# Moving elementwise work between three engines: layer 0's mixers, the S5 state exchange and layer 1's qkv

## The chip, the cores and the metric

One core of one Trainium2 chip runs the whole program. The metric is the device time of one execution in microseconds (us). The core has a matrix engine (TensorE, PE in the profile; its weight loads are PEld), a vector engine (VectorE, DVE), an activation engine (ScalarE, ACT), a general engine (GpSimd, POOL) and a queue that issues most transfers (SyncE, SP). Each takes its own instructions in program order; they meet at semaphores.

## The reference

Two layers of a transformer-like trunk run on 1024 latent tokens and 256 context tokens of width 1024. Layer 0 has one input projection that feeds two mixers, an S5 state-space scan and a gated linear attention (GLA), both in both directions; layer 1 has grouped-query attention with rotary positions. Each layer ends in a squared-ReLU MLP of width 4096.

```python
def even_mixer(h, ...):                       # layer 0
    u, q, k, v, r, glr = split(h @ w_in)      # S5 input, GLA q/k/v/r, gate rank
    s5  = s5_bidir(u, ...)                    # hs[t] = lam_bar * hs[t-1] + b_bar @ u[t], both ways
                                              # y = Re(C @ hs) + d*u ; g = gelu(y) ; g * sigmoid(g @ w_glu + b)
    gla = gla_bidir(q, k, v, r, glr, ...)     # g = log_sigmoid(glr @ w_gate2 + b)/16, chunks of 64:
                                              # b = cumsum(g); o = (q e^b) S + tril((q e^b)(k e^-b)^T) v
                                              # S = S e^bl + (k e^(bl-b))^T v ; rms_norm(o) * silu(r)
    return concat(s5, gla) @ w_out
# layer 1: q,k,v = h @ w_qkv; rms_norm, rope on latents; softmax over latent + context keys; @ w_o
# both:    x += gate * mixer ; x += gate * (relu(h @ w1)**2 @ w2)
```

## The kernel before

**Numbers.** All matrix products are made from two-part operands: `hi`, a copy of x in a narrower format (ACT writes it), and `lo = x - hi` (an elementwise subtraction). A dense product is three passes, hi·hi, lo·hi, hi·lo (L404 to L406), so every weight and every activation needs its subtraction before PE can take it. `wload` (L226 to L238) loads a weight (SP, L235), makes hi (ACT, L236) and lo (L237); by default lo is made on POOL, and its callers in `mixer_half`, `mixer_out` and the first group of `qkv` ask for DVE. `split` (L381) alternates POOL and DVE, `affine` (L388) has POOL in three of four.

**Layer 0 up to its output projection.** The token tiles are 512 + 512 latent and 256 context tokens. Independent pieces of work are written as generators and are interleaved with the dense projections of qk, v, r and glu; a list scheduler then fixes the order of every engine's instructions before the run.

- S5: tables (`s5_tables`, L652 to L681: products on DVE L652 to L654 and on POOL L656 to L658, stored to `cld` and `kd`), input products (`s5_in`, complex products by `cmul` L415 to L422, every third on POOL; L755 to L761), then the scan. In the scan every eighth state column is chained serially (`s5_chain`, 38 steps of three small DVE instructions, L813, L817, L818), and the columns between are filled by `s5_join` (one product L790 and two additions L795 for each call of 40 columns). There are eight pairs (un, d) of joins; in the last, (3, 1), POOL does them with a temporary `tm2`, in the other seven DVE with `tmp`.
- S5 output (`s5_out`): per un, loads issued by POOL (L855 to L858), an exchange of state quarters for each d (ACT L863, DVE L864, ACT L865), products L880 and L882, gelu L884, a store to `gd`, and the glu projection.
- GLA: `gla_gates` makes for each of 4 groups and 3 token tiles the decay tiles: matrix product L1000, ACT L1002, L1004, L1005, DVE L1003, POOL L1006, a DVE scan (L1009 or L1011), ACT exponentials L1014 to L1016 and L1019, DVE L1017 and L1020, POOL L1021 and L1022, stores to `qkd` and `wkd`. `gla_first` loads `wkd` back, transposes (L1067), multiplies (L1078) and accumulates the chunk states on DVE (L1091); `gla_second` makes the outputs (L1191 to L1197, one product L1196 on POOL).

Weights of the dense projections rotate through a ring of three buffers; a weight is loaded only when the product three loads back is finished. The first weight of the output projection (`w_out_e`, tile number 274) follows the glu weights in that ring.

**Layer 1.** `qkv` loads nine weight groups and applies `rope_tile` (L1735 to L1742: shuffle, product on POOL L1740, product and sum on DVE L1741, L1742). The MLP-down weights (L1463) and the attention's splits keep their POOL instructions in both versions.

Of the kernel before, what the change touches and what calls it, by code (L numbers as in the profile page):

```python
# [222 lines left out]
    s.A.free(*s.wr)  # L223


def wload(s, src, n=1024, eng=None, own=False):  # L226

    nc = s.nc
    hi, lo = [s.A([n], F32R) for _ in range(2)] if own else (s.wr[0](), s.wr[1]())
    st = s.A.f32(lo)  # L230
    shp = list(src.shape)
    dst = st[:, :n]
    if len(shp) == 3:
        dst = dst.rearrange("p (a b) -> p a b", a=shp[1])
    nc.sync.dma_start(dst, src)  # L235
    nc.scalar.activation(hi[:, :n], st[:, :n], AF.Copy)  # L236
    (eng or nc.gpsimd).tensor_tensor(lo[:, :n], st[:, :n], hi[:, :n].bitcast(F32), OP.subtract)  # L237
    return hi, lo  # L238


# [140 lines left out]
def split(s, hi, lo, src, k=0):  # L381

    nc = s.nc
    nc.scalar.activation(hi, src, AF.Copy)
    (nc.gpsimd if k % 2 else nc.vector).tensor_tensor(lo, src, hi.bitcast(F32), OP.subtract)


def affine(s, t, a, b, hi, lo, k):  # L388

    nc = s.nc  # L390
    nc.scalar.activation(hi, t, AF.Identity, bias=b, scale=a)  # L391
    nc.vector.tensor_scalar(t, t, a, b, OP.mult, OP.add)
    (nc.vector if k % 4 == 0 else nc.gpsimd).tensor_tensor(lo, t, hi.bitcast(F32), OP.subtract)  # L393


def dense(s, w, kt, act, n, off=0, mw=128, ms=128, kind="mm"):
# [135 lines left out]
def s5_prep(s):  # L532
# [61 lines left out]
    w1, w2 = A([16, 16], top=True), A([16, 16], top=True)  # L594
    for d in range(2):
        cfb = [cf[:, i, 16 * d:16 * d + 16, None].to_broadcast([128, 16, 16]) for i in range(2)]
        cmul(nc.gpsimd, Bb[:, 0, 16 * d:16 * d + 16], Bb[:, 1, 16 * d:16 * d + 16], cfb,
             [t.B[:, 0], t.B[:, 1]], w1, w2)

    s.pin = A([2, 32, 8])  # L600
# [36 lines left out]
def s5_tables(s):  # L637
# [6 lines left out]
    for st in range(8):  # L644
        un, b = divmod(st, 2)
        CL = cl()
        for d in range(2):
            g0 = 16 * d + 2 * st
            P = [s.pout[:, j, g0:g0 + 2, :, None].to_broadcast(sh) for j in range(2)]
            C = [s.Ct[:, j, 2 * st:2 * st + 2, None, :].to_broadcast(sh) for j in range(3)]  # L650
            e = nc.vector
            e.tensor_tensor(tw[0], P[1], C[1], OP.mult)  # L652
            e.tensor_tensor(CL[:, 0, d], P[0], C[0], OP.mult)
            e.tensor_tensor(CL[:, 0, d], CL[:, 0, d], tw[0], OP.subtract)  # L654
            e = nc.gpsimd
            e.tensor_tensor(CL[:, 1, d], P[0], C[2], OP.mult)  # L656
            e.tensor_tensor(tw[1], P[1], C[0], OP.mult)
            e.tensor_tensor(CL[:, 1, d], CL[:, 1, d], tw[1], OP.subtract)  # L658
        for j in range(2):
            nc.sync.dma_start(s.cld[un][64 * j:64 * j + 64, 1152 * b:1152 * b + 1152]  # L660
                              .rearrange("p (e x) -> e p x", e=2), CL[:, j].rearrange("p d g k c -> p (d g k c)"))
        yield 1.0
        tb = tab()
        pd = []
        for d in range(2):
            p = ps(s, "sp")
            nc.vector.memset(p[:, 0:128], 0.0)
            pd.append(p)
            for q in range(4):
                e, g2 = q % 2, q // 2  # L670
                h = slice(64 * e, 64 * e + 64)
                for j in range(2):
                    nc.tensor.matmul(p[32 * q:32 * q + 16, 0:128], s.Bb[h, j, 16 * d + 2 * st + g2, :],
                                     CL[h, j, d, g2, d:d + 8].rearrange("p a b -> p (a b)"),
                                     start=(j == 0), stop=(j == 1))
        nc.scalar.activation(tb[:, 0:112], pd[1][:, 0:112], AF.Copy)
        nc.scalar.activation(tb[:, 112:240], pd[0][:, 0:128], AF.Copy)
        k0 = tb[:, 112:128]
        nc.vector.tensor_tensor(k0, pd[1][:, 112:128], k0, OP.add)
        nc.vector.scalar_tensor_tensor(k0, s.eye16, s.dsk[:, st:st + 1], k0, OP.mult, OP.add)  # L680
        nc.sync.dma_start(s.kd[un, b], tb)  # L681
        yield 1.0
# [11 lines left out]
def s5_in(s):  # L694
# [12 lines left out]
    def weights(g2):  # L707
        wt, t1, t2 = wtr(), tr[0](), tr[1]()
        a = [pin[:, j, :, g2, :, None].to_broadcast(sh) for j in range(2)]
        b = [Bb[:, j, :, g2, None, :].to_broadcast(sh) for j in range(2)]  # L710
        cmul(nc.gpsimd if g2 % 3 == 0 else nc.vector, wt[:, 0], wt[:, 1], a, b, t1, t2)
        return wt

    def transposes(g2, wt):
# [25 lines left out]
    for g2 in range(16):  # L740
# [9 lines left out]
        for d in range(2):  # L750
# [6 lines left out]
            if d == 0:  # L757
                nc.scalar.activation(H[0][:, g2, :, 1:160], pv[:, :, 0:159], AF.Copy)
            else:
                nc.vector.tensor_copy(H[1][:, g2, :, 0:159], pv[:, :, 1:160])  # L760
            nc.vector.tensor_copy(fin[:, :, d, g2], pv[:, :, 160 + d])  # L761
        yield 0.6
        if g2 % 4 == 3:
# [34 lines left out]
def s5_chain(s):  # L798
# [29 lines left out]
    tmp, tm2 = A([640]), A([640])  # L828
    for un in range(4):
        for d in range(2):  # L830
            e, t = (nc.gpsimd, tm2) if (un, d) == (3, 1) else (v, tmp)
            s5_join(s, e, t, un, d, 4, 2, 0, 40)
            s5_join(s, e, t, un, d, 2, 1, 0, 80)
            yield 2.0
# [9 lines left out]
def s5_out(s):  # L844
# [7 lines left out]
    def load(un):  # L852
# [6 lines left out]
        for d in range(2):  # L859

            a, b = s.H[d][64:128, 4 * un:4 * un + 4, 0], s.H[d][0:64, 4 * un:4 * un + 4, 1]
            t = swr()[0:64]
            nc.scalar.activation(t, a, AF.Copy)  # L863
            nc.vector.tensor_copy(a, b)  # L864
            nc.scalar.activation(b, t, AF.Copy)  # L865

    load(0)
    load(1)
# [110 lines left out]
def gla_gates(s):  # L979
# [7 lines left out]
    for hp in range(2):  # L987
        for tb, (t0, n, _) in enumerate(TBS):
# [7 lines left out]
            for d in range(2):  # L996
# [6 lines left out]
                v.tensor_scalar(mm, z[:, :n], bg, 0.0, OP.add, OP.min)  # L1003
                nc.scalar.activation(a, a, AF.Exp, scale=-1.0)  # L1004
                nc.scalar.activation(a, a, AF.Ln, bias=1.0)  # L1005
                nc.gpsimd.tensor_tensor(mm, mm, a, OP.subtract)  # L1006
                b, r, w = a, s.rst[:, :n], mm
                if d == 0:
                    v.tensor_tensor_scan(b, r, mm, 0.0, OP.mult, OP.add)  # L1009
# [8 lines left out]
                                OP.subtract)  # L1018
                nc.scalar.activation(w, w, AF.Exp, scale=IT)  # L1019
                v.scalar_tensor_tensor(e, e, 0.125, q, OP.mult, OP.mult)  # L1020
                nc.gpsimd.tensor_tensor(f, f, k, OP.mult)  # L1021
                nc.gpsimd.tensor_tensor(w, w, k, OP.mult)  # L1022
                for h in range(2):
                    for i, x in enumerate((e, f)):
                        nc.sync.dma_start(s.qkd[hp][64 * d:64 * d + 64, h, i, t0:t0 + n], x[64 * h:64 * h + 64])
# [75 lines left out]
def gla_second(s, hm):  # L1101
# [63 lines left out]
    def finish(u):  # L1165
# [21 lines left out]
        for h in range(2):  # L1187
# [5 lines left out]
            for j in range(m):  # L1193
                col_bcast(s, pb, rs[:, m * h + j:m * h + j + 1], j)
            v.scalar_tensor_tensor(os[h][:, :n], os[h][:, :n], s.gla_norm, pb[:, :n], OP.mult, OP.mult)
            nc.gpsimd.tensor_tensor(os[h][:, :n], os[h][:, :n], rt[:, h, :n], OP.mult)  # L1196
            split(s, *acts(hm[tb])(4 + 2 * hp + h), os[h][:, :n])  # L1197
        A.free(rs)
        if hp == 1:
# [180 lines left out]

def mixer_half(s, l, w_src, h):

    nc = s.nc
    wsrc = w_src.rearrange("(k p) m -> p k m", p=128)
    for j in range(4):
        w = wload(s, wsrc[:, 0:4, 256 * j:256 * j + 256], eng=nc.vector)
        for tb in range(3):
            for i in range(2):
                p = dense(s, w, 4, acts(h[tb]), TBS[tb][1], off=128 * i, ms=256)
# [3 lines left out]
def mixer_out(s, l, w_src, key, part, h, ready):  # L1393
# [8 lines left out]
    s.done -= {("h", 0), ("h", 1), ("h", 2), ("cols", 0), ("cols", 1)}  # L1402
    accs = [sums(s, tb) for tb in range(3)]
    if l == 0:
        kept = [wload(s, wsrc[:, 4:8, 256 * j:256 * j + 256], eng=nc.vector, own=True) for j in range(4)]

    def weights(m):
        if l == 0:
            w = kept[m // 2]
            return lambda tb: dense(s, w, 4, lambda k: acts(h[tb])(4 + k), TBS[tb][1], off=128 * (m % 2), ms=256)  # L1410
        w = wload(s, wsrc[:, :, 128 * m:128 * m + 128], eng=nc.vector)
        return lambda tb: dense(s, w, KT, acts(h[tb]), TBS[tb][1])

    for tbs in ((2, 0), (1,)):
# [320 lines left out]
def rope_tile(s, out, x, t0, n):  # L1735
# [1 line left out]
    nc = s.nc  # L1737
    sw = s.qt()
    nc.vector.stream_shuffle(sw[:, :n], x, [i ^ 1 for i in range(32)])
    nc.gpsimd.tensor_tensor(out, x, s.rope[0][:, t0:t0 + n], OP.mult)  # L1740
    nc.vector.tensor_tensor(sw[:, :n], sw[:, :n], s.rope[1][:, t0:t0 + n], OP.mult)  # L1741
    nc.vector.tensor_tensor(out, out, sw[:, :n], OP.add)  # L1742

# [16 lines left out]
def qkv(s, h):  # L1760
# [98 lines left out]

    tiles = [(do_k, 0, 8), (do_k, 1, 9), (do_v, 0, 10), (do_v, 1, 11)] + [(do_q, i, i) for i in range(8)]  # L1860
    for gi, grp in enumerate((tiles[0:4],) + tuple(tiles[i:i + 1] for i in range(4, 12))):
        ws = [wload(s, wsrc[:, :, 128 * c:128 * c + 128], eng=nc.vector if gi == 0 else None) for _, _, c in grp]
        for tb in range(3):
            drain(s, ("h", tb))
            for (fn, i, c), w in zip(grp, ws):
# [505 lines left out]
```

## Time and profile before

| quantity | value |
|---|---|
| device time, median of 3 runs | 3262.33 us (3258.59 to 3269.24) |
| the profiled execution | 3259.84 us |
| its span in the trace | 3257.5 us |
| PE busy | 3045.1 us, 93% of the span |
| DVE busy | 2244.2 us, 69% |
| ACT busy | 1332.9 us, 41% |
| POOL busy | 728.1 us, 22% |

The span lies 2.34 us inside the time of the profiled execution, which lies 2.49 us below the median. The shares are means over stages with different limits, so they have to be read stage by stage: the joins of the scan run up to 493 us, the first S5 output product starts at 529.88 us, the output projection fills the time to 800 us, and qkv lies at 1640 to 1900 us. POOL's 728 us are in layer 0's first 570 us, in the splits of the MLP-down weights and in layer 1.

### The profile page before, as it was taken

Reading aid. Unit: us, or ns where it says so; the run is one execution under the profiler, and the core shown is the slowest. Engines: PE = TensorE matmul, PEld = TensorE weight load, DVE = VectorE, ACT = ScalarE, POOL = GpSimd, SP = SyncE. Lnnn points to the kernel's source line nnn. Section 1 sums busy time; section 2 is a strip of 40 time slices with the busy share of each in tenths; the row PEclk is TensorE's granted clock in tenths of the full one; section 3 lists DMA queues with packets and bytes.
Section 4 is the critical chain, followed back from the end, with each engine's and each line's share of the span. In section 5 each row is a group of like instructions: output and inputs, shape, how many; then the busy total and the mean of one; then the engine's idle time right before and its main releaser. Section 6 shows DMA issues by size and latency. Waiting matters only on the chain. (4 is left out here: it accounts for less than half of the span.)

```text
span 3257.5 us, 48482 instructions
## 1 busy us (share of the span) xinstructions
PE 3045.1 (93%) x17458; PEld 2552.3 (78%) x17458; DVE 2244.2 (69%) x4290; ACT 1332.9 (41%) x2485; POOL 728.1 (22%) x659
## 2 busy tenths in 40 slices
PE   7987876999999999999987999999999999999998
PEld 4665555887788887777776878888888888888887
DVE  4576993557876575766885467777478665768778
ACT  4321422423533353433332257777435333444432
POOL 3443452010000013343402212121000000144442
PEclk9988887999999999999988989999999999999999
DMA  9532668533443456646431210100435444534424
GB/s 330 144 90 86 189 206 244 196 117 107 139 139 127 138 196 203 210 154 202 127 107 38 76 33 16 36 14 16 130 117 159 143 134 138 185 117 129 146 94 155
DMA packets 402080, 433.89 MB, mean 133 GB/s; under 512 B 45704, under 2 KB 286816, under 8 KB 396208
## 3 DMA queue, kind: packets, MB, share of 16 engines
q1 hardware_dynamic: 398704, 418.66, 40.2%
q0 software_dynamic: 3136, 12.13, 1.2%
q8 instruction: 138, 2.26, 0.3%
q14 instruction: 102, 0.84, 0.1%
HBM read 296.78 MB, written 133.92 MB: 132 GB/s over the span
## 5 line engine op out<-in xcount | busy, mean ns | idle before, releaser
L1453 PE MATMUL banks<-sb_512r 128*128 128x512 f32 x5376 | 1261.2, 391 | 19.4 <-DVE sb L1651 9.9
L1453 PEld LDWEIGHTS banks<-sb_512r 128*128 128x128 f32 x5376 | 997.5, 188 | 244.2 <-DVE sb L1651 17.4
L1462 ACT ACTIVATE sb_512r<-sb 128x512 fp32r<-128x512 f32 x786 | 482.2, 630 | 816.4 <-DMA sb<-in_w_mlp_out 233.7
L1463 POOL TENSOR_TENSOR sb_512r<-sb,sb_512r 128x512 fp32r<-128x512 f32 x256 | 352.3, 1404 | 1417.7 <-DVE sb L1442 519.0
L1463 DVE TENSOR_TENSOR sb_512r<-sb,sb_512r 128x512 fp32r<-128x512 f32 x530 | 387.5, 761 | 53.1 <-ACT sb_512r L1462 49.5
L1651 DVE TENSOR_TENSOR sb<-sb,banks 128x512 f32<-128x512 f32 x472 | 317.2, 681 | 140.5 <-PE banks L1453 131.2
L404 PE MATMUL banks<-sb_512r,sb_1024r 128*128 128x512 f32 x640 | 263.0, 411 | 12.0 <-ACT sb_512r L391 6.7
L406 PE MATMUL banks<-sb_512r,sb_1024r 128*128 128x512 f32 x640 | 258.1, 405 | 1.3 <-POOL sb_512r L393 1.1
L405 PE MATMUL banks<-sb_512r,sb_1024r 128*128 128x512 f32 x640 | 258.8, 405 | 0.0
L1962 DVE TENSOR_TENSOR sb_1024r<-banks,sb_1024r 128x512 fp32r<-128x512 f32 (+1 forms) x208 | 136.4, 664 | 53.3 <-ACT sb_1024r L1961 52.0
L1937 ACT ACTIVATE sb<-banks,sb,sb 128x512 f32<-128x512 f32 (+1 forms) x208 | 157.2, 764 | 21.4 <-DVE sb L1934 20.4
L1925 DVE TENSOR_REDUCE sb<-banks 128x1 f32<-128x512 f32 (+1 forms) x208 | 136.6, 664 | 33.8 <-PE banks L1924 31.9
L404 PEld LDWEIGHTS banks<-sb_512r,sb_1024r 128*128 128x128 f32 x640 | 125.2, 196 | 43.0 <-ACT sb_512r L391 7.7
L1477 PE MATMUL banks<-sb_256r,sb_512r 128*128 128x256 f32 x512 | 147.6, 289 | 6.1 <-DVE sb_512r L1463 6.1
L1476 PE MATMUL banks<-sb_256r,sb_512r 128*128 128x256 f32 x512 | 147.1, 288 | 5.6 <-ACT sb_512r L1462 5.6
L406 PEld LDWEIGHTS banks<-sb_512r,sb_1024r 128*128 128x128 f32 x640 | 123.8, 193 | 36.0 <-POOL sb_512r L393 3.8
L405 PEld LDWEIGHTS banks<-sb_512r,sb_1024r 128*128 128x128 f32 x640 | 124.8, 195 | 30.2 <-issue 6.8
L1476 PE MATMUL banks<-sb_512r 128*128 128x256 f32 x512 | 145.8, 285 | 1.3 <-ACT sb_512r L1462 1.3
L1478 PE MATMUL banks<-sb_256r,sb_512r 128*128 128x256 f32 x512 | 146.8, 287 | 0.0
L1477 PE MATMUL banks<-sb_512r 128*128 128x256 f32 x512 | 145.1, 283 | 0.0
L1478 PE MATMUL banks<-sb_512r 128*128 128x256 f32 x512 | 144.6, 283 | 0.0
L1961 ACT ACTIVATE sb_1024r<-banks 128x512 fp32r<-128x512 f32 (+1 forms) x208 | 118.4, 583 | 63.9 <-PE banks L1958 60.6
(372 smaller groups left out, 5753.5 us busy)
## 6 DMA issues: line engine op xcount, KB each, us to landing
md<-sb SPq DMA_DIRECT2D x256, 256.0 KB
sb<-md SPq DMA_DIRECT2D x256, 256.0 KB
sb<-in_w_mlp_in SPq DMA_DIRECT2D x168, 256.0 KB
sb<-in_w_ada SPq DMA_DIRECT2D x40, 1024.0 KB
sb<-in_w_mlp_out SPq DMA_DIRECT2D x128, 256.0 KB
sb<-xd SPq DMA_DIRECT2D x72, 256.0 KB
xd<-sb SPq DMA_DIRECT2D x48, 256.0 KB
sb<-in_w_in_e SPq DMA_DIRECT2D x16, 512.0 KB
```

Of the source, the lines that this page charges most:

```text
L404: nc.tensor.matmul(p[:mw, :n], hi[:, a:b], xh, start=(k == 0), stop=False)
L405: nc.tensor.matmul(p[:mw, :n], lo[:, a:b], xh, start=False, stop=False)
L406: nc.tensor.matmul(p[:mw, :n], hi[:, a:b], xl, start=False, stop=(k == kt - 1))
L1453: nc.tensor.matmul(bank, x[:, o], y, start=first and k == 0 and i == 0, stop=last and k == len(B) - 1 and i == 2, skip_group_check=True)
L1462: s.nc.scalar.activation(hi, raw, AF.Copy)
L1463: e.tensor_tensor(lo, raw, hi.bitcast(F32), OP.subtract)
L1476: nc.tensor.matmul(o, hi, xh, start=(k == 0), stop=False)
L1477: nc.tensor.matmul(o, lo, xh, start=False, stop=False)
L1478: nc.tensor.matmul(o, hi, xl, start=False, stop=(k == n - 1))
L1651: v.tensor_tensor(d, d, x, OP.add)
L1925: v.tensor_reduce(m[:, kb:kb + 1], p, AX.X, OP.max)
L1937: nc.scalar.activation(P[:, 512 * i:512 * i + w], p, AF.Exp, bias=m[:, 4:5], scale=sc, accum_out=m[:, 6 + i:7 + i])
```

## The change

Every elementwise instruction that layer 0's mixers, the weight loads, `split`, `affine` and `rope_tile` gave to POOL goes to DVE. The copy of the second direction's states in `s5_in` (L760) goes from DVE to ACT. The two copies of the exchange (L863, L865) go from ACT to DVE. The last pair of joins goes to DVE, and the two directions use the two temporaries. POOL keeps its DMA issues. Line numbers after the change are one lower from L655 on and two lower from L1383 on.

```diff
@@ wload
-    (eng or nc.gpsimd).tensor_tensor(lo[:, :n], st[:, :n], hi[:, :n].bitcast(F32), OP.subtract)
+    nc.vector.tensor_tensor(lo[:, :n], st[:, :n], hi[:, :n].bitcast(F32), OP.subtract)
@@ split
-    (nc.gpsimd if k % 2 else nc.vector).tensor_tensor(lo, src, hi.bitcast(F32), OP.subtract)
+    nc.vector.tensor_tensor(lo, src, hi.bitcast(F32), OP.subtract)
@@ affine
-    (nc.vector if k % 4 == 0 else nc.gpsimd).tensor_tensor(lo, t, hi.bitcast(F32), OP.subtract)
+    nc.vector.tensor_tensor(lo, t, hi.bitcast(F32), OP.subtract)
@@ s5_prep
-        cmul(nc.gpsimd, Bb[:, 0, 16 * d:16 * d + 16], Bb[:, 1, 16 * d:16 * d + 16], cfb,
+        cmul(v, Bb[:, 0, 16 * d:16 * d + 16], Bb[:, 1, 16 * d:16 * d + 16], cfb,
@@ s5_tables
-            e = nc.gpsimd
             e.tensor_tensor(CL[:, 1, d], P[0], C[2], OP.mult)
@@ s5_in
-        cmul(nc.gpsimd if g2 % 3 == 0 else nc.vector, wt[:, 0], wt[:, 1], a, b, t1, t2)
+        cmul(nc.vector, wt[:, 0], wt[:, 1], a, b, t1, t2)
-                nc.vector.tensor_copy(H[1][:, g2, :, 0:159], pv[:, :, 1:160])
+                nc.scalar.activation(H[1][:, g2, :, 0:159], pv[:, :, 1:160], AF.Copy)
@@ s5_chain
-            e, t = (nc.gpsimd, tm2) if (un, d) == (3, 1) else (v, tmp)
+            e, t = (v, (tmp, tm2)[d])
@@ s5_out
-            nc.scalar.activation(t, a, AF.Copy)
+            nc.vector.tensor_copy(t, a)
             nc.vector.tensor_copy(a, b)
-            nc.scalar.activation(b, t, AF.Copy)
+            nc.vector.tensor_copy(b, t)
@@ gla_gates
-                nc.gpsimd.tensor_tensor(mm, mm, a, OP.subtract)
+                nc.vector.tensor_tensor(mm, mm, a, OP.subtract)
-                nc.gpsimd.tensor_tensor(f, f, k, OP.mult)
-                nc.gpsimd.tensor_tensor(w, w, k, OP.mult)
+                nc.vector.tensor_tensor(f, f, k, OP.mult)
+                nc.vector.tensor_tensor(w, w, k, OP.mult)
@@ gla_second
-            nc.gpsimd.tensor_tensor(os[h][:, :n], os[h][:, :n], rt[:, h, :n], OP.mult)
+            nc.vector.tensor_tensor(os[h][:, :n], os[h][:, :n], rt[:, h, :n], OP.mult)
@@ rope_tile
-    nc.gpsimd.tensor_tensor(out, x, s.rope[0][:, t0:t0 + n], OP.mult)
+    nc.vector.tensor_tensor(out, x, s.rope[0][:, t0:t0 + n], OP.mult)
```

The scheduler places the moved instructions anew. On DVE, in the serial chain of the scan, before: gate instructions stand between the chain's three (the chain's state tile is 10240_87, the gate tiles are 512_20xx).

```order
564 L817 TENSOR_TENSOR sb_10240_87<-sb_10240_87,sb_128_115 128x2x2x16
565 L818 TENSOR_TENSOR sb_10240_87<-sb_10240_87,sb_128_115 128x2x2x16
566 L813 TENSOR_TENSOR sb_128_2017<-sb_10240_87,sb_128_808 128x128
567 L1009 SCALAR_TENSOR_TENSOR sb_512_2063<-sb_512_2056,sb_512_2065 128x256
568 L817 TENSOR_TENSOR sb_10240_87<-sb_10240_87,sb_128_2017 128x2x2x16
569 L1017 TENSOR_TENSOR sb_512_2065<-sb_512_2063 128x256
570 L818 TENSOR_TENSOR sb_10240_87<-sb_10240_87,sb_128_2017 128x2x2x16
571 L1003 TENSOR_SCALAR sb_512_2066<-banks,sb_48_272 128x256
```

And in the changed kernel, on DVE in the same place:

```order
610 L817 TENSOR_TENSOR sb_10240_87<-sb_10240_87,sb_128_2019 128x2x2x16
611 L1019 SCALAR_TENSOR_TENSOR sb_512_2067<-sb_512_2067,sb_1024_2062 128x512
612 L1020 TENSOR_TENSOR sb_512_2069<-sb_512_2069,sb_1024_2062 128x512
613 L812 TENSOR_TENSOR sb_128_115<-sb_10240_87,sb_128_808 128x128
614 L1005 TENSOR_TENSOR sb_512_2066<-sb_512_2066,sb_512_2064 128x512
615 L1021 TENSOR_TENSOR sb_512_2065<-sb_512_2065,sb_1024_2062 128x512
616 L816 TENSOR_TENSOR sb_10240_87<-sb_10240_87,sb_128_115 128x2x2x16
617 L1010 SCALAR_TENSOR_TENSOR sb_512_2064<-sb_512_2056,sb_512_2066 128x512
```

The three instructions of each gate tile that POOL had (L1005, L1020, L1021 by the new numbers) now stand between the steps of the chain.

The second place is the first weight of the output projection (L237 on tile 274). On DVE before, it stands behind the last join, among the GLA state sums (L1091) and the last exchanges (L864):

```order
714 L795 TENSOR_TENSOR sb_10240_87<-sb_10240_87,sb_640_2584 128x2x4x40 x2
715 L1060 MEMSET sb_1024_3476 128x128
716 L1091 SCALAR_TENSOR_TENSOR sb_1024_3476<-sb_1024_3476,sb_40_2059,banks 128x128 x3
717 L1091 SCALAR_TENSOR_TENSOR sb_128_3473<-sb_1024_3476,sb_40_2059,banks 128x128
718 L1091 SCALAR_TENSOR_TENSOR sb_1024_3474<-sb_1024_3474,sb_40_2059,banks 128x128 x3
719 L288 TENSOR_TENSOR sb_96_101<-sb_512_796,sb_96_100 128x32
720 L353 SCALAR_TENSOR_TENSOR sb_16_5436<-sb_96_101,sb_48_272 128x16
721 L237 TENSOR_TENSOR sb_1024r<-sb_1024_274,sb_1024r 128x1024
```

In the changed kernel it stands on DVE among the joins of the second pair of four (L789, L794), with the exchange (L862 to L864) between them and no L1090 yet:

```order
825 L789 TENSOR_TENSOR sb_640_2585<-sb_10240_87,sb_128_806 128x640
826 L794 TENSOR_TENSOR sb_10240_87<-sb_10240_87,sb_640_2584 128x2x4x40
827 L794 TENSOR_TENSOR sb_10240_87<-sb_10240_87,sb_640_2585 128x2x4x40
828 L237 TENSOR_TENSOR sb_1024r<-sb_1024_274,sb_1024r 128x1024
829 L794 TENSOR_TENSOR sb_10240_87<-sb_10240_87,sb_640_2584 128x2x4x40
830 L794 TENSOR_TENSOR sb_10240_87<-sb_10240_87,sb_640_2585 128x2x4x40
831 L862 COPY sb_640_3964<-sb_10240_87 64x640
```

What moved: the weight's subtraction has joins and exchanges queued behind it. Six such subtractions stand between the first chain step and the end of the joins.

The third place is PE, just ahead of the first S5 output product (L882 before, L881 after). Before:

```order
1567 L1067 MATMUL banks<-sb_400_61,sb_512_3466 128x128 x4
1568 L1078 MATMUL banks<-sb_1024_3467,sb_512_3472 64x128 x14
1569 L1067 MATMUL banks<-sb_400_61,sb_512_3466 128x128 x2
1570 L1078 MATMUL banks<-sb_1024_3470,sb_512_3471 64x128 x16
1571 L1067 MATMUL banks<-sb_400_61,sb_512_3465 128x128 x4
1572 L882 MATMUL banks<-sb_10240_87,sb_2304_3961 128x160 x2
```

After, on PE:

```order
1569 L1077 MATMUL banks<-sb_1024_3469,sb_512_3471 64x128 x8
1570 L1066 MATMUL banks<-sb_400_61,sb_512_3465 128x128 x4
1571 L1077 MATMUL banks<-sb_1024_3469,sb_512_3472 64x128 x8
1572 L281 MATMUL banks<-sb_400_61,sb_512_796 128x128 x4
1573 L1077 MATMUL banks<-sb_1024_3468,sb_512_3471 64x128 x16
1574 L1066 MATMUL banks<-sb_400_61,sb_512_3465 128x128 x2
1575 L1066 MATMUL banks<-sb_400_61,sb_512_3466 128x128 x4
1576 L881 MATMUL banks<-sb_10240_87,sb_2304_3961 128x160 x2
```

Ahead of the first output product stand 62 products of L1077 where 92 of L1078 stood; all of them come behind the dense projections but for four transposes.

## Rows read from the trace of the kernel before

**Rows 1.** Windows: start:end, length, then busy us and count per engine, PE clock, DMA.

```profile
100.00:326.00 226.00, 185.33 (x1343) 146.77 (x1341) 146.38 (x367) 48.16 (x94) 101.94 (x115) 0.90 0.35 93
326.00:493.00 167.00, 136.87 (x701) 92.56 (x701) 160.71 (x254) 62.00 (x128) 85.74 (x71) 0.86 0.66 198
493.00:530.00 37.00, 16.81 (x131) 13.50 (x132) 12.94 (x36) 10.88 (x15) 5.80 (x11) 0.50 0.86 263
571.00:800.00 229.00, 220.78 (x1398) 192.92 (x1397) 144.49 (x314) 80.90 (x140) 16.52 (x14) 0.98 0.43 141
1640.00:1900.00 260.00, 230.97 (x1251) 200.17 (x1249) 150.26 (x361) 79.42 (x138) 48.95 (x29) 0.90 0.20 64
```

**Rows 2.** Waits, 326 to 493 us: engine, line, waited for; us, times, longest.

```profile
PE banks L1000 <- DVE sb L1003: 9.1, 2, 7.2
```

**Rows 3.** DVE's lines, 326 to 493 us: count, busy us, mean ns, idle before.

```profile
L795 DVE TENSOR_TENSOR sb<-sb,sb 128x320 f32<-128x320 f32 x42 | 33.1, 789 | 0.8
L790 DVE TENSOR_TENSOR sb<-sb,sb 128x640 f32<-128x640 f32 x21 | 27.3, 1302 | 0.4
L813 DVE TENSOR_TENSOR sb<-sb,sb 128x128 f32<-128x128 f32 x38 | 21.2, 558 | 1.0
L817 DVE TENSOR_TENSOR sb<-sb,sb 128x64 f32<-128x64 f32 x38 | 20.1, 530 | 0.9
L818 DVE TENSOR_TENSOR sb<-sb,sb 128x64 f32<-128x64 f32 x38 | 17.1, 451 | 0.9
L1020 DVE SCALAR_TENSOR_TENSOR sb<-sb,sb 128x512 f32<-128x512 f32 x8 | 8.6, 1077 | 2.2 <-ACT sb L1015 2.2
...
L1091 DVE SCALAR_TENSOR_TENSOR sb<-sb,sb,banks 128x128 f32<-128x128 f32 x15 | 5.0, 336 | 0.0
```

**Rows 4.** Timeline of all engines, 401 to 403 us: start us, us, engine, line.

```profile
401.98 1.28 POOL L1021 TENSOR_TENSOR sb<-sb,sb 128x512 f32<-128x512 f32 x1
...
402.02 1.79 DVE L1017 TENSOR_TENSOR sb<-sb 128x512 f32<-128x512 f32 x1
```

**Rows 5.** Single lines over the whole span: count, then min/median/max ns.

```profile
L817 DVE TENSOR_TENSOR sb<-sb,sb x38: 235/273/2348, 327.5 to 413.5; 128x64 f32<-128x64 f32 x38
L813 DVE TENSOR_TENSOR sb<-sb,sb x38: 364/382/1400, 326.6 to 413.0; 128x128 f32<-128x128 f32 x38
L864 DVE COPY sb<-sb x8: 486/487/603, 474.0 to 521.3; 64x640 f32<-64x640 f32 x8
L393 DVE TENSOR_TENSOR sb_256r<-sb,sb_256r x26: 410/416/861, 98.4 to 2405.7; 128x256 fp32r<-128x256 f32 x26
L393 DVE TENSOR_TENSOR sb_512r<-sb,sb_512r x20: 678/686/1667, 40.5 to 1699.1; 128x512 fp32r<-128x512 f32 x20
L237 DVE TENSOR_TENSOR sb_1024r<-sb,sb_1024r x28: 1206/1225/1477, 509.0 to 2414.8; 128x1024 fp32r<-128x1024 f32 x28
L237 POOL TENSOR_TENSOR sb_1024r<-sb,sb_1024r x26: 2341/2382/2924, 33.1 to 1832.2; 128x1024 fp32r<-128x1024 f32 x26
```

**Rows 6.** DVE's timeline, joins with POOL idle.

```profile
484.57 1.33 DVE L790 TENSOR_TENSOR sb<-sb,sb 128x640 f32<-128x640 f32 x1
...
486.82 0.74 DVE L795 TENSOR_TENSOR sb<-sb,sb 128x320 f32<-128x320 f32 x1
...
488.61 0.85 DVE L790 TENSOR_TENSOR sb<-sb,sb 128x640 f32<-128x640 f32 x1
...
490.11 1.02 DVE L795 TENSOR_TENSOR sb<-sb,sb 128x320 f32<-128x320 f32 x2
```

**Rows 7.** Waits, 493 to 530 us.

```profile
PE banks L1067 <- DMA sb<-wkd: 13.6, 2, 11.1
```

**Rows 8.** Timeline of all engines, 507 to 530 us.

```profile
507.95 1.06 ACT L236 ACTIVATE sb_1024r<-sb 128x1024 fp32r<-128x1024 f32 x1 [9.36 <-DMA sb<-in_w_out_e]
...
529.88 1.27 PE L882 MATMUL banks<-sb,sb 128*128 128x160 f32 x4
```

**Rows 9.** Waits, 100 to 326 us.

```profile
PE banks L755 <- DVE sb L679: 12.9, 4, 5.4
```

More of the change, by code (lines that the diff above doesn't have):

```diff
@@ L223, in w_free, with wload @@
     s.A.free(*s.wr)
-def wload(s, src, n=1024, eng=None, own=False):
+def wload(s, src, n=1024, own=False):
     nc = s.nc
@@ L1381, in mixer_half @@
 def mixer_half(s, l, w_src, h):
-    nc = s.nc
     wsrc = w_src.rearrange("(k p) m -> p k m", p=128)
     for j in range(4):
-        w = wload(s, wsrc[:, 0:4, 256 * j:256 * j + 256], eng=nc.vector)
+        w = wload(s, wsrc[:, 0:4, 256 * j:256 * j + 256])
         for tb in range(3):
@@ L1404, in mixer_out @@
     if l == 0:
-        kept = [wload(s, wsrc[:, 4:8, 256 * j:256 * j + 256], eng=nc.vector, own=True) for j in range(4)]
+        kept = [wload(s, wsrc[:, 4:8, 256 * j:256 * j + 256], own=True) for j in range(4)]
     def weights(m):
@@ L1410, in weights @@
             return lambda tb: dense(s, w, 4, lambda k: acts(h[tb])(4 + k), TBS[tb][1], off=128 * (m % 2), ms=256)
-        w = wload(s, wsrc[:, :, 128 * m:128 * m + 128], eng=nc.vector)
+        w = wload(s, wsrc[:, :, 128 * m:128 * m + 128])
         return lambda tb: dense(s, w, KT, acts(h[tb]), TBS[tb][1])
@@ L1861, in qkv @@
     for gi, grp in enumerate((tiles[0:4],) + tuple(tiles[i:i + 1] for i in range(4, 12))):
-        ws = [wload(s, wsrc[:, :, 128 * c:128 * c + 128], eng=nc.vector if gi == 0 else None) for _, _, c in grp]
+        ws = [wload(s, wsrc[:, :, 128 * c:128 * c + 128]) for _, _, c in grp]
         for tb in range(3):
```

## The prediction

> **What bounds the kernel now.** I read the table of busy shares first: PE is busy for 93% of the span, so only the stretches in which PE waits can give time back, and POOL's work is worth something only where DVE or PE waits beside it. The windows then give the stretches [rows 1]. From 326 to 493 us, where the serial chain and the joins of the S5 scan run, DVE is busy 160.71 of 167 us and PE only 136.87: DVE sets the end of this stretch. The waits confirm it from PE's side: the gates' product waits 9.1 us for a DVE instruction [rows 2]. From 493 to 530 us every engine idles (PE 16.81 of 37 us): this is latency, GLA state steps one after another, and 13.6 us of PE's idle time end with a load of wkd [rows 7]. The first S5 output product comes at 529.88 us [rows 8]. From 571 us PE is busy 220.78 of 229 us, so whatever is won or lost before then is carried to the end. In the tables' stretch, 100 to 326 us, DVE has 80 us to spare (146.38 of 226), and PE still waits for it at places, 12.9 us for one line [rows 1, 9]. In qkv PE is busy 230.97 of 260 us.
>
> Next I read single durations. DVE's small chain instructions have a median of 273 and 382 ns over the span but a mean of 530, 451 and 558 ns in this stretch [rows 3, 5]. The timeline shows why: with POOL's 1.28 us instruction beginning at 401.98, a DVE instruction begun at 402.02 lasts 1.79 us [rows 4], where another instruction of 512 columns has a median of 0.686 us [rows 5]. DVE stands still while POOL works beside it, and that is in its busy time.
>
> **The change, part by part.** All sums go against the profiled execution, 3259.84 us (span 3257.5 us and 2.34 us around it); the median of the runs is 2.49 us above it.
>
> Stretch of chain and joins (326 to 493 us). What goes from DVE's busy time is the stretching beside POOL. Chain: 38 × (558 − 382) = 6.7, 38 × (530 − 273) = 9.8, and for L818, which has L817's shape, 38 × (451 − 273) = 6.8 us: 23.3 [rows 3, 5]. Joins: a pair (un, d) has one L790 and two L795 at stride 4, and two L790 and four L795 at stride 2. Undisturbed that is 1.33 + 2 × 0.74 + 2 × 0.85 + 2 × 1.02 = 6.55 us [rows 6]; seven pairs make 45.9, and the rows have 33.1 + 27.3 = 60.4 [rows 3]: 14.5. L1020: 8 × (1077 − 686) = 3.1. Together 40.9 us. What comes: three instructions for each gate tile, eight tiles of 512 columns at 0.686 and four of 256 at 0.416, 16.5 + 5.0 = 21.5 [rows 3, 5]; six weight subtractions of 1.225, 7.4; the eighth pair, 6.55; sixteen exchange copies of 0.487, taken from L864, which has their shape, 7.8, and the four of L864 that come after 493 us now, 1.9. Together 45.2. What moves behind: the 15 state sums L1091, 5.0 [rows 3]. So 160.7 − 40.9 + 45.2 − 5.0 = 160.0 us: the saturated engine takes all of POOL's work and ends where it was. The exchange is then already done, where four of eight were left before.
>
> New waits come with it. DVE now waits itself for ACT in each gate tile, where POOL did, with chain instructions queued behind. The trace shows no such wait for the three moved instructions; the nearest row is L1020, which waits for ACT in the same tile and lost 2.2 us in eight tiles [rows 3]. Bounds: 0 and, with three times that and twice over for the smaller cover, 13 us. I take 4.4, twice the row, because the order puts chain instructions between a tile's three. The joins end at 493 + 4 = 497 us, by −7 to +13.
>
> From the joins to S5's output (37 us). PE had 92 L1078 products queued ahead of its first output product and has 62 afterwards, all behind the joins; of the 92 a part was done among the joins, so that some 54 remained after 493 us (counted from the order by where the joins end). The work is about the same; but the transposes now run several steps ahead, so that the reloads of wkd (13.6 us of waiting) can be in before they are needed. Bounds: 0 and −13.6; I take −12, since the gates that make wkd are finished no later than before while its consumers come later. It is the step that I know least.
>
> Tables (100 to 326 us). POOL's 101.94 us become about half on DVE: L237 takes 2.382 us on POOL and 1.225 on DVE, a ratio of 0.51, so 52 us come. If POOL stretched DVE here as it did in the next stretch (40.9 us for 85.74 of POOL, 0.48), 49 us go. DVE stays inside its 226 us. PE's waits for DVE are 12.9 us at L679; POOL's products in the same chain of stores halve. I take −4; bounds −13 (the row) and +15 (nothing of the stretching goes beyond DVE's 80 idle us, and the tables come later by a third of the net addition).
>
> 571 to 800 us: L1196 is the only POOL product, 16.52 us of POOL; PE covers it: −1, bounds −3 and 0. qkv: 48.95 us of POOL become 25 on DVE, which has 110 us idle, less 23 of stretching: 0, bounds −6 and +6. L760 goes to ACT, which has 178 of 226 us idle: 0.
>
> Sum: +4 − 12 − 4 − 1 = −13 us: 3259.84 − 13 = 3247, and by the runs' median 3249 us.
>
> The Trainium skill has a rule that speaks about this exchange, "SBUF — State Buffer", section "SBUF: two separate sides": VectorE and GpSimd share a port pair that is held for a whole instruction, and the other one blocks fully. By that alone up to all 85.74 us that POOL worked would have been paid by DVE, and the stretch would shorten by 85.7 − 45.2 = 40 us; the 1.79 us instruction agrees with the rule, but the rows sum to 40.9 us of stretching, so about half of POOL's time was paid for.
>
> **The rivals.**
>
> A: a weight blocks the queue (slower). In the order after, the subtraction for the output projection's first weight stands among the second un's joins with five pairs (5 × 6.55 = 33 us) and the exchange copies (8 us) queued behind it, 41 us in all. Its ACT copy comes only when the weight has landed; before, that was 507.95 + 1.06 = 509.0 us [rows 8], after the ring buffer was given back by a dense product. If the dense projections end no earlier than before, DVE stands from 497 − 41 = 456 until 509, the joins end at 509 + 1.2 + 41 = 551 instead of 497, and the time is 3249 + 54 = 3303. Each microsecond beyond 456 counts; after 13 of them the gain is gone. For it: DVE takes instructions in order, and the wait of 9.36 us for this weight stands in the rows. Against: in the new order the dense products nearly all precede the GLA steps on PE, and the joins and gates that held them end no later, so that I estimate the weight at 456 to 474 us. The full price is then unlikely, a part of it is not.
>
> B: no change. The 12 us are not won, because the wkd reloads or the stores queued on SP come when they came, and the waits in the gates cost what the tables win: 3262 ± 6.
>
> C: more. The tables' waits go in full (13 instead of 4) and the gates' waits are nothing (4): 3249 − 13 = 3236, and with both lower bounds of the joins' end 3229.
>
> D: DVE is only loaded further. The Trainium skill says this, "Perfetto Trace Analysis", section "Optimizing Scalar/DVE Operations": with a saturated DVE, work may be moved off it, though between DVE and GpSimd that might not help because of the shared port; here the work moves the other way. As a mechanism of this kernel: were the chain's stretching not POOL's doing but caused by dependent instructions waiting for each other's writes, nothing of the 40.9 would go, and the stretch would end 41 + 4 us later: 3262 − 17 + 45 = about 3290. Against it stands the pair in the timeline [rows 4].
>
> **How the numbers follow.** Two times closer than 0.3% (9.8 us) cannot be told apart with this kernel: faster means below 3252.5, slower above 3272. Forecast 0.43 (own range 3236 to 3262; three quarters of it below 3252.5), B 0.20, C 0.12, A 0.20 (in part or in full), D 0.05. Faster: 0.32 + 0.12 + 0.03 = 0.47. Same: 0.11 + 0.16 + 0.01 = 0.28. Slower: A and D, 0.25. The range goes down to C with some of the tables' lower bound, 3216, and up to A in part, 3290; A's full price stays outside.
>
> **What would show it.** Right: L813, L817, L818 at their medians of 382 and 273 ns as means; joins at 6.55 us a pair; DVE's busy time from the chain's start to the joins' end still near 160 us; first S5 output product near 521 us; no wkd wait of 11 us on PE. Wrong: DVE idle for tens of microseconds before L237 with joins behind it (A); means of the chain unchanged (D); the output product at 530 with PE waiting for wkd (B); PE's wait for L679 gone and the chain starting ten us earlier (C). qkv would be wrong if PE's 29 idle us there grew.

## The result: slower by 0.9%, and the profile after

The changed kernel takes 3290.73 us (median of 4 runs, 3286.72 to 3298.25) against 3260.46 for the kernel before; the ratio is 1.0091, with a 95% interval of 1.0062 to 1.0120. The forecast was 3249 us, faster. Its profiled execution took 3286.72 us, its span is 3284.9 us.

The first half went at least as well as forecast. These are windows of the changed kernel, with the columns of [rows 1]:

```profile
100.00:326.00 226.00, 193.65 (x1459) 157.18 (x1461) 154.45 (x459) 55.29 (x116) 1.50 (x6) 0.93 0.35 97
326.00:493.00 167.00, 112.91 (x528) 72.36 (x520) 145.91 (x310) 54.20 (x113) 15.94 (x29) 0.79 0.67 206
493.00:530.00 37.00, 24.58 (x198) 20.55 (x199) 12.54 (x38) 6.40 (x11) 2.47 (x5) 0.60 0.65 204
571.00:800.00 229.00, 217.46 (x1371) 189.81 (x1370) 136.22 (x303) 74.80 (x127) 1.83 (x2) 0.95 0.40 133
```

From 326 to 493 us DVE does all of POOL's work and is busy for 145.91 us where it was busy for 160.71 [rows 1]. Its lines there show why (count, busy us, mean ns, idle before; compare [rows 3]):

```profile
L794 DVE TENSOR_TENSOR sb<-sb,sb 128x320 f32<-128x320 f32 x48 | 24.8, 562 | 0.3
L789 DVE TENSOR_TENSOR sb<-sb,sb 128x640 f32<-128x640 f32 x24 | 22.6, 973 | 0.1
L812 DVE TENSOR_TENSOR sb<-sb,sb 128x128 f32<-128x128 f32 x38 | 14.7, 388 | 0.6
L816 DVE TENSOR_TENSOR sb<-sb,sb 128x64 f32<-128x64 f32 x38 | 10.3, 271 | 0.6
...
L1019 DVE SCALAR_TENSOR_TENSOR sb<-sb,sb 128x512 f32<-128x512 f32 x8 | 5.5, 685 | 4.6 <-ACT sb L1014 4.1 <-DMA sb<-qd 0.5
```

The chain's means fell from 558 and 530 ns to 388 and 271, the undisturbed durations. Eight pairs of joins take 24.8 + 22.6 = 47.4 us, less than seven took before (60.4). The first S5 output product comes at 519.70 us, 10.2 us earlier than in [rows 8]:

```profile
519.70 1.43 PE L881 MATMUL banks<-sb,sb 128*128 128x160 f32 x4 [4.51 <-DMA sb<-cld]
```

The loss is beside it. From 326 to 493 us PE is busy for 24 us less than before (112.91 against 136.87), and the timeline of PE shows one hole:

```profile
431.56 0.28 PE L406 MATMUL banks<-sb_256r,sb_1024r 128*128 128x256 f32 x1
...
444.90 2.83 PE L879 MATMUL banks<-sb,sb 128*128 128x160 f32 x6 [1.70 <-DMA sb<-kd]
489.58 1.98 PE L1077 MATMUL banks<-sb,sb 64*64 64x128 f32 x32 [41.85 <-ACT sb L1068]
```

The dense projections are finished at 432 us, 59 us earlier than before, where their last product is this one:

```profile
490.20 0.42 PE L406 MATMUL banks<-sb_256r,sb_1024r 128*128 128x256 f32 x1
```

After a few smaller products PE then stands for 41.85 us, from 448 us until GLA's first state product. The waits from 426 to 500 us say what it stands for:

```profile
PE banks L1077 <- ACT sb L1068: 41.8, 1, 41.8
ACT sb L1068 <- DVE sb L794: 38.1, 1, 38.1
```

PE waits for ACT's copy of GLA's first transposed tile (L1068), and this copy waits for an addition of the S5 joins (L794). The two compute nothing for each other. They meet in memory. The kernel's allocator gives `tm2` the columns 38928 to 39568, and after the joins have been written in the program it gives `gla_first`'s two transposed tiles the columns 38864 to 39888. In the kernel before, `tm2` served only POOL's pair of joins, done by 457 us; in the changed kernel every join of the second direction uses it, up to 488 us. So no GLA state step can run before the last join. Before, 15 state sums ran among the joins [rows 3]; now none does.

Followed by line: GLA's last state product starts at 574.6 us (560.1 before), the first sum of squares of GLA's outputs (L1182) at 603.2 (583.1), the first column sum behind layer 0's output projection (L1257) at 769 (754), qkv's first column sum (L1753) at 1724.3 (1711.5) and its last at 1922.7 (1900.9), and the span ends 27.4 us later. The S5 path won 10 us and GLA, which ends last, lost 14 and then 20. Of the whole loss 13 us are there when qkv begins, 9 come in qkv and some 6 behind it.

PE's clock adds to it. Rows of PE in the changed kernel just behind the last state sum:

```profile
581.14 0.80 PE L404 MATMUL banks<-sb_2048r,sb_1024r 128*128 128x512 f32 x1 [2.15 <-ACT sb_2048r L384]
581.73 0.63 PE L405 MATMUL banks<-sb_2048r,sb_1024r 128*128 128x512 f32 x1
...
583.14 2.07 PE L1138 MATMUL banks<-sb 64*128 64x128 f32 x8
```

A 512-column product of L405 takes 0.63 us here and 0.40 from 597 us on; the granted clock between 580 and 600 us is 0.56 where the kernel before had 1.00. That is near the lower of the two levels (1.2 of 2.4 GHz), after a stretch (560 to 580 us) in which PE was busy 12.85 of 20 us. The price can be read where both kernels have the same products in the same order. From GLA's first output product to the end of the second group of state terms (L1161, L1162 before), the changed kernel takes 9.4 us:

```profile
588.30 1.22 PE L1156 MATMUL banks<-sb,sb 128*128 128x128 f32 x4
...
595.88 1.81 PE L1161 MATMUL banks<-sb,sb 128*128 128x64 f32 x8
```

The kernel before takes 5.5 us, so 3.9 of the 20 us are the clock's in these products alone:

```profile
576.29 0.71 PE L1157 MATMUL banks<-sb,sb 128*128 128x128 f32 x4
...
580.82 1.00 PE L1162 MATMUL banks<-sb,sb 128*128 128x64 f32 x8
```

### The profile page after: what moved, and what is told of

Its sections match the earlier page's. It is cut to its first block, busy times and chain, and to the rows that moved or that the text cites. A ratio compares the mean times of both kernels' runs of the same rounds, so it can differ in the third digit from the quotient of the medians.

```text
span 3284.9 us, 48397 instructions
## 1 busy us (share of the span) xinstructions
PE 3053.6 (93%) x17458; PEld 2558.4 (78%) x17458; DVE 2252.6 (69%) x4508; ACT 1328.7 (40%) x2485; POOL 461.7 (14%) x441
## 5 line engine op out<-in xcount | busy, mean ns | idle before, releaser
L404 PE MATMUL banks<-sb_512r,sb_1024r 128*128 128x512 f32 x640 | 259.8, 406 | 12.3 <-ACT sb_512r L391 5.8
L405 PE MATMUL banks<-sb_512r,sb_1024r 128*128 128x512 f32 x640 | 257.4, 402 | 0.0
L406 PE MATMUL banks<-sb_512r,sb_1024r 128*128 128x512 f32 x640 | 254.6, 399 | 1.4 <-DVE sb_512r L393 1.4
L1475 PE MATMUL banks<-sb_256r,sb_512r 128*128 128x256 f32 x512 | 145.9, 285 | 4.1 <-DVE sb_512r L1461 4.1
L1474 PE MATMUL banks<-sb_512r 128*128 128x256 f32 x512 | 145.9, 285 | 1.0 <-ACT sb_512r L1460 1.0
L405 PEld LDWEIGHTS banks<-sb_512r,sb_1024r 128*128 128x128 f32 x640 | 123.6, 193 | 25.7 <-issue 2.5
```

The source lines that it names most:

```text
L404: nc.tensor.matmul(p[:mw, :n], hi[:, a:b], xh, start=(k == 0), stop=False)
L405: nc.tensor.matmul(p[:mw, :n], lo[:, a:b], xh, start=False, stop=False)
L406: nc.tensor.matmul(p[:mw, :n], hi[:, a:b], xl, start=False, stop=(k == kt - 1))
L1474: nc.tensor.matmul(o, hi, xh, start=(k == 0), stop=False)
L1475: nc.tensor.matmul(o, lo, xh, start=False, stop=False)
```

## The experiments

The kernel before takes 3269 to 3273 us on the chips on which these ran, and 3260 us on the first; each ratio is to the kernel before on the same chip. One temporary, a temporary apart, the joins alone and qkv back ran on a second chip, the two kernels once more, both repairs and the gates on a third, the other three on a fourth. In the kernels with a temporary apart the line numbers from there on are one higher than in the changed kernel.

**The changed kernel and the one before, once more, on one chip.**

> The changed kernel once more, on the same chip as its variants: a ratio to the kernel before of 1.006 to 1.012 as on the first chip. Theory M (memory): one temporary (1.0055 before) wins little over it and the temporaries apart (0.9985) win 0.7 to 1.2%. If the changed kernel is at 1.005 or less here, the first chip's 0.9% had a part that the kernel does not explain.

Measured: 1.0066 (1.0050 to 1.0083), 3295.73 us. The wait is there again (35.8 us of ACT's copy for L794, 42.4 us of PE).

> The kernel before once more, for a trace from the chip on which the experiments run: its stages are expected where the first trace has them (first S5 output product 530, GLA output sums from 583, output projection from 754 us), later by up to 12 us if this chip's transfers are slower, since its runs here have a median of 3271.8 where the first chip had 3260.5 us.

Measured: 3273.32 us. The stages come at 535, 590 and 765 us: 5 to 12 us later than on the first chip. The rows that the next verdicts are compared with, GLA's state products and the S5 output products of the two (count, min/median/max ns, first to last start us), the kernel before first, then the changed one:

```profile
L1078 PE MATMUL banks<-sb,sb x304: 268/415/473, 463.1 to 569.6; 64*64 64x128 f32 x152
...
L882 PE MATMUL banks<-sb,sb x128: 298/300/633, 534.7 to 573.9; 128*128 128x160 f32 x128
```

```profile
L1077 PE MATMUL banks<-sb,sb x304: 268/414/474, 496.4 to 582.8; 64*64 64x128 f32 x152
...
L881 PE MATMUL banks<-sb,sb x128: 298/300/634, 528.0 to 571.3; 128*128 128x160 f32 x128
```

**One temporary.** In the changed kernel no join uses `tm2`:

```diff
-            e, t = (v, (tmp, tm2)[d])
+            e, t = (v, tmp)
```

> The changed kernel with one edit: all eight pairs of joins use the temporary tmp, and tm2 is used by none. Theory M (memory): gla_first's two transposed tiles lie on the addresses of tm2, which the change keeps in use up to the last join, so the first ACT copy of a transposed tile waits for the joins (38.1 us in the changed kernel's trace). Without a user of tm2 the first L1077 starts before 455 us instead of 489.6, 14 or 15 of the L1090 run among the joins, and the last of them ends near 563 instead of 577; the time falls by 12 to 20 us, to 3271 to 3279. Theory Q (queue): DVE's work in its order is the bound there, and the wait for the temporary is only how it shows: the time stays at 3291 +- 4.

Measured: 1.0055 (1.0036 to 1.0073), 3287.98 us, which the interval does not tell from the changed kernel's 1.0066. The start moved as theory M said, the time did not:

```profile
L1077 PE MATMUL banks<-sb,sb x304: 269/269/473, 435.7 to 576.4; 64*64 64x128 f32 x152
```

The first state product comes at 435.7 us, but the recurrence stops after 15 sums. The longest wait of PE from 446 to 530 us is now

```profile
PE banks L1077 <- DVE sb L1090: 42.3, 2, 41.5
```

for a state sum that stands behind the last join in DVE's order. The third of GLA's state tiles has the columns 35792 to 36816, and `tmp` 35728 to 36368: the other temporary lies under GLA's tiles as well. Half of the theory's cure was thus no cure. The last state sum starts at 587.4 us, not near 563, and the time is where theory Q put it.

The kernel before has this second overlap too. On DVE there, the memset of the third state tile (L1060) and the 16th state sum come right behind the last join:

```profile
492.02 1.02 DVE L795 TENSOR_TENSOR sb<-sb,sb 128x320 f32<-128x320 f32 x2
493.14 0.17 DVE L1060 MEMSET sb<- 128x128 f32 x1
493.40 1.56 DVE L1091 SCALAR_TENSOR_TENSOR sb<-sb,sb,banks 128x128 f32<-128x128 f32 x4
```

So one temporary puts GLA back to where the kernel before had it, 15 sums ahead of the last join. The time does not come back, because the joins, with the 15 sums between them again, now end at 509 us (493 and 498 in the two traces of the kernel before).

**A temporary apart.** The same, and the one temporary at columns that `gla_first` does not use (`small=True` is new in the allocator and takes them from the area of small tiles):

```diff
-    tmp, tm2 = A([640]), A([640])
+    A.free(prr, pp2)
+    tmp = A([640], small=True)
...
-            e, t = (v, (tmp, tm2)[d])
+            e, t = (v, tmp)
...
-    A.free(prr, pp2, tmp, tm2, s.cc, s.s5L)
+    A.free(tmp, s.cc, s.s5L)
```

> The changed kernel with one temporary for all joins, at addresses that gla_first does not use (in the small area of memory, over the chain's temporaries, which are freed first). Theory M: no GLA tile waits for a join; about 30 L1090 more come among the joins and the exchange, the first L881 starts at about 505 us instead of 519.7, the last L1090 ends before 555, and the time falls by 25 to 40 us to 3251 to 3266. Theory Q: 3291 +- 4.

Measured: 0.9985 (0.9972 to 0.9998), 3267.81 us, 2 us above theory M's range. Against the changed kernel that is 0.9985/1.0066, 0.8% or some 27 us less. Against one temporary (1.0055), on the same chip and with the same instructions on the same engines, it is 20 us less; only the columns of memory differ, and the order that the scheduler makes from them:

```profile
L1078 PE MATMUL banks<-sb,sb x304: 269/417/473, 434.6 to 543.2; 64*64 64x128 f32 x152
...
L882 PE MATMUL banks<-sb,sb x128: 299/299/635, 522.9 to 557.1; 128*128 128x160 f32 x128
```

State products and joins interleave, and the last state product starts at 543.2 instead of 582.8 us. The first S5 output product is not the 505 us that was expected: the joins, with GLA's sums between them, end at 517 us. From 446 to 520 us DVE is busy for 63 of 74 us, which speaks for DVE as the next limit. Theory Q, which had no gain here, falls as it stood. But this cure takes away more than the change had brought in, since the kernel before has the overlap of `tmp` with the third state tile as well. The same repair was not run on the kernel before, so what it would win there is not known.

**The joins alone.** In the kernel before, only the pair (3, 1) goes to DVE, and the two temporaries are used in turn.

> The kernel before with one edit: the pair of joins (3,1) goes from POOL to DVE and the directions use tmp and tm2 in turn; everything else stays where it was. Theory M: the transposed tiles wait for the last join here too, no L1091 comes before the joins' end, and the time rises by 10 to 25 us to 3270 to 3286. Theory Q: only 6.5 us of DVE work come and 14 of stretching go, so 3260 +- 6.

Measured: 1.0009 (0.9994 to 1.0023). Theory M's 10 to 25 us do not come, though the first state product moves to the joins' end as it said:

```profile
L1078 PE MATMUL banks<-sb,sb x304: 269/320/473, 488.7 to 567.2; 64*64 64x128 f32 x152
```

The time stays, as theory Q had it. PE waits only 9.1 us for the copy here, since the dense projections run until 480 us (432 in the changed kernel). But a short wait of PE is not why the overlap is free. The recurrence is held back as long as in the changed kernel, which the way from the end of the last join to the start of the last state sum shows (all on DVE, us; the first two on the first chip, the next two on the third, the others on the second):

| kernel | last join ends | last state sum starts | between |
|---|---|---|---|
| before | 493.0 | 562.7 | 69.7 |
| changed | 488.9 | 577.1 | 88.2 |
| before, once more | 497.7 | 572.2 | 74.5 |
| changed, once more | 495.7 | 585.2 | 89.5 |
| the joins alone | 487.9 | 575.4 | 87.5 |
| changed, qkv back (below) | 496.7 | 584.4 | 87.7 |
| one temporary | 508.8 | 587.4 | 78.6 |
| a temporary apart | 517.0 | 545.8 | 28.8 |

With all sums behind the joins 88 us are left, with 15 of them ahead 70 to 79. In this run the joins end some 10 us earlier than in the kernel before (traced on another chip), and that pays for it. In the changed kernel, with the rest of POOL's work on DVE, they end only 2 to 4 us earlier; with qkv back, on the chip of this run, 9 us later than here. So the overlap and DVE's work act together, and neither theory is right alone.

**qkv back.** In the changed kernel, layer 1's rope product and the weight subtractions of qkv's groups 1 to 8 are on POOL again:

```diff
-    nc.vector.tensor_tensor(out, x, s.rope[0][:, t0:t0 + n], OP.mult)
+    nc.gpsimd.tensor_tensor(out, x, s.rope[0][:, t0:t0 + n], OP.mult)
...
-        ws = [wload(s, wsrc[:, :, 128 * c:128 * c + 128]) for _, _, c in grp]
+        ws = [wload(s, ..., eng=nc.vector if gi == 0 else nc.gpsimd) for _, _, c in grp]
```

> The changed kernel with layer 1's qkv as before: rope's product and the weight subtractions of its groups 1 to 8 on POOL again. If DVE is what qkv lost by (its first to last product took 189.4 us before and 198.4 after), the time falls by 9 us to 3282 and the stretch is back at 189 to 191. If the 9 us are only a shifted order or a shifted clock, the time stays within 3 us of 3291.

Measured: 1.0048 (1.0031 to 1.0065), 3287.27 us; qkv's stretch, first to last column sum, is 191 us (1739 to 1930), against 196 in the changed kernel on these chips (1736 to 1932) and 190 in the one before. So qkv did lose to DVE, though this ratio alone does not show it.

**Both repairs.** The temporary apart, and qkv back on POOL.

> Both repairs: one temporary apart from gla_first's tiles, and layer 1's qkv on POOL as before. If the two losses are separate, they add: the temporaries apart gave 0.9985 and qkv's stretch lost 7 to 9 us (0.2 to 0.3%), so 0.995 to 0.997, faster than the kernel before. If qkv's loss only follows from what comes ahead of it, 0.998 to 1.000.

Measured: 0.9959 (0.9945 to 0.9974), 3259.22 us: faster than the kernel before by 0.4%, as it would be if the two losses add. PE's longest wait in qkv, ahead of the dense products, was in the kernel with the temporary apart and in this one

```profile
PE banks L404 <- ACT sb L1748: 9.1, 3, 5.0
```

```profile
PE banks L404 <- ACT sb L1748: 4.6, 3, 3.8
```

**Which part of qkv.** From the kernel with the temporary apart, only rope's product back on POOL, then only the weights:

> The kernel with the temporaries apart (0.9985) and rope's product alone on POOL again. Both parts of qkv back gave 0.9959. If rope's 20 products (13.9 us of DVE) are what qkv lost by, 0.995 to 0.997 and PE's 9.2 us of waiting at the head of the dense products fall to 5; if the weight subtractions are, 0.998 to 0.999.

> The same kernel with only the weight subtractions of qkv's groups 1 to 8 on POOL again (8 x 1.225 = 9.8 us off DVE). If they stand in DVE's queue ahead of what PE waits for, 0.995 to 0.997; if rope is the cause, 0.998 to 0.999. If neither alone gives more than half, the two share one limit of DVE.

Measured: 0.9998 (0.9983 to 1.0012) and 0.9987 (0.9973 to 1.0001). In the traces the stretch is 195 and 190 us, against 193 with neither and 189 with both, which speaks for the weights; but PE's wait for L1748 is 9.6 and 9.2 us in the two, and the ratios show no gain from either. Inconclusive: only both together show one.

**Gates back on POOL.** From the kernel with the temporary apart, the three instructions of each gate tile on POOL.

> One temporary apart, and the three instructions of each gate tile on POOL again. If POOL stretches DVE by 0.48 us for each of its own (as worked out from the trace of before), 47 us of POOL cost 23 us of DVE and save 21.5: the first S5 output product stays within 4 us and the ratio within 0.002 of 0.9985. If the stretching has another cause, the 21.5 us come off DVE: the first output product 15 to 20 us earlier, ratio 0.993 to 0.995.

Measured: 0.9995 (0.9982 to 1.0008), first output product 523.7 us instead of 522.9: as the first alternative said. This is the test of the stretching. One of the chain's lines, from 326 to 520 us, with the gates on POOL and with them on DVE:

```profile
L816 DVE TENSOR_TENSOR sb<-sb,sb 128x64 f32<-128x64 f32 x38 | 16.9, 444 | 0.8
```

```profile
L816 DVE TENSOR_TENSOR sb<-sb,sb 128x64 f32<-128x64 f32 x38 | 10.3, 271 | 0.6
```

The same 38 instructions take 6.6 us more once POOL works beside them again. The chain's other two lines, again with the gates on POOL and then on DVE:

```profile
L812 DVE TENSOR_TENSOR sb<-sb,sb 128x128 f32<-128x128 f32 x38 | 21.8, 574 | 0.9
L817 DVE TENSOR_TENSOR sb<-sb,sb 128x64 f32<-128x64 f32 x38 | 17.7, 465 | 0.8
```

```profile
L812 DVE TENSOR_TENSOR sb<-sb,sb 128x128 f32<-128x128 f32 x38 | 14.7, 386 | 0.6
L817 DVE TENSOR_TENSOR sb<-sb,sb 128x64 f32<-128x64 f32 x38 | 10.3, 270 | 0.6
```

Together the chain takes 21.1 us more. What DVE saves by giving the gates away (21.5 us) it pays back in such stretching.

**Exchange back on ACT.** From the kernel with both repairs, the exchange's two copies on ACT:

> The kernel with both repairs (0.9959) and the exchange's two copies on ACT again. If DVE's work up to the last exchange sets the first S5 output product (524 us), 7.8 us come off it: first product at 516 to 520, ratio 0.993 to 0.995. If the handing over between ACT and DVE costs as much (before, ACT waited 12.3 us in four of the copies), or if GLA's recurrence is the limit, 0.995 to 0.997.

Measured: 0.9955 (0.9940 to 0.9971); the first output product at 520.2 us instead of 524.0. The S5 output starts 4 us earlier, as the first alternative had it at its least; the ratio does not move by what can be told. So the exchange looks to be off the path that decides.

## Why the prediction was wrong

The stretching: right, and larger than worked out. The terms of the chain hit (388 and 271 ns as means); the joins were undisturbed at 47.4/8 = 5.9 us a pair instead of 6.55. DVE was busy for 145.9 us, not 160, and the joins ended at 489 us, not 497. (The bounds given for that end, −7 to +13, do not follow from the waits' bounds of 0 and 13 us, which make −4 to +9.) The gate experiment shows POOL as its cause, so rival D's premise falls.

New waits in the gates: 4.4 us were taken; DVE waited 4.1 us for ACT at L1019 and 2.7 at L1002. Right in size.

Rival A: DVE did wait for the weight among the joins, but 4.6 us over all six subtractions. The dense work was finished at 432 us, and the weight came early, as the argument against A had it.

From the joins to S5's output: the first product came at 519.7, forecast 521. The number was right by luck, and for a path that no longer decided: the joins ended 8 us earlier than forecast and the way from there took 31 us, not 25.

The step that failed is "What moves behind: the 15 state sums L1091, 5.0", together with "whatever is won or lost before then is carried to the end". The first credits DVE with 5 us and charges nothing. But the sums are steps of GLA's serial recurrence, and the kernel's first stage ends when both the recurrence and S5's output have ended. Moved behind the joins, they left 88 us of the recurrence to do after the last join instead of 70. The joins ended only 4 us earlier, so the recurrence ended 14 us later, while S5's last gelu (L883, L884 before) came 7 us earlier. Nor was all carried to the end: of the 20 us that GLA's outputs came later, 13 are left when qkv begins. In the order of the changed kernel all L1090 stood behind the joins; that was read, and taken for a saving. That memory holds the sums behind the joins is what the temporary apart showed: 20 us against one temporary, with every instruction still on its engine. That the second temporary's overlap alone made the loss is not shown. Taking it out of the changed kernel (one temporary) and putting it into the kernel before (the joins alone) both left the time where it was. The measured 3290.73 us is also the price of rival D, about 3290, and the upper end of the range; that is chance, since D's mechanism did not occur.

Tables, 100 to 326 us: −4 was taken; the chain started 1.2 us later than before. PE's wait for L679 went from 12.9 to 0.8 us, but its wait for ACT's copies (L676, L677 before) rose from 3.6 to 12.5 us. The rows after:

```profile
PE banks L754 <- ACT sb L676: 12.5, 2, 7.6
...
PE banks L754 <- DVE sb L678: 0.8, 1, 0.8
```

qkv: 0 was taken, with bounds of ±6; its stretch grew by 9 us on the first chip (189 to 198) and by 6 on the other (190 to 196). DVE's 110 idle us in it did not cover what came. This is the second term that failed: 9 of the 27 us.

With the temporary apart and qkv left on POOL, the kernel is 13.5 us faster than the one before (3259.22 against 3272.76). That this is near the −13 of the sum is luck: two of its terms, the tables and the way from the joins to S5's output, came out otherwise, and the repair also takes away an overlap that the kernel before has.

What stays open: what the temporary apart would win in the kernel before, and so what moving the work is worth by itself; how the loss in qkv splits between rope and the weights; how much of the 20 us at GLA's outputs is the lower clock beyond the 3.9 us read above; and where the 6 us behind qkv come from.

## What to carry to other kernels

An edit that moves work between engines also moves the lifetime of the temporaries: see which later tiles get their columns, for a wait between two unrelated lines (ACT's copy for a join's addition) is a reuse of memory. Where two paths meet in one end, charge a delayed step to its own path before crediting the engine that it leaves. And the length of a wait is not its price: PE waited 9.1 us for the same copy in one kernel and 41.8 in the other, and in both the recurrence had 88 us to go behind the joins.

## What the runs showed of the hardware

A DVE instruction with two inputs in on-chip memory is stretched many times over beside POOL: 0.27 us at the median and 2.35 at most for one of 64 columns [rows 5]. In the kernel before, that longest one ends 0.13 us after the POOL instruction that began just ahead of it:

```profile
385.26 2.38 POOL L237 TENSOR_TENSOR sb_1024r<-sb,sb_1024r 128x1024 fp32r<-128x1024 f32 x1 [0.73 <-ACT sb_1024r L236]
385.42 2.35 DVE L817 TENSOR_TENSOR sb<-sb,sb 128x64 f32<-128x64 f32 x1
```

In the changed kernel, with no elementwise work on POOL beside the chain, the chain's two additions (L816 and L817 now) take at most 0.31:

```profile
L816 DVE TENSOR_TENSOR sb<-sb,sb x38: 241/273/309, 328.2 to 426.1; 128x64 f32<-128x64 f32 x38
L817 DVE TENSOR_TENSOR sb<-sb,sb x38: 241/272/306, 328.5 to 426.4; 128x64 f32<-128x64 f32 x38
```

The 36 gate instructions, some 47 us on POOL in the trace of before, cost the kernel nothing that can be told on either engine.
